# Transposes moved into the next quad's first product, and operand loads held back behind a deep transfer queue

## The chip, the cores and the metric

The kernel runs on one core of a Trainium2 chip. Its time is the device time of one execution in microseconds (us). A core has five engines that run side by side, each with its own instruction stream in order: PE multiplies matrices into PSUM, DVE does elementwise work on whole tensors, ACT does elementwise functions (and copies with a scale), POOL here mostly starts transfers that add while they write, and SP starts the plain transfers. PE's weight loads stand in the profile as a stream of their own (PEld). An instruction that needs another engine's result, or a buffer that another engine still reads, waits at the head of its stream, and everything behind it waits with it.

## The reference

One layer of an encoder trunk over 512 tokens of 2048 channels, in float32: an adaLN modulation computed from c, a token mixer (an RG-LRU group and a pooling group), and a SwiGLU network with 5632 hidden channels. The part that the change touches is the last one:

```
h = modulate(rmsnorm(x, g_norm_ffn), sh2, sc2)
f = (silu(h @ w_ffn_gate) * (h @ w_ffn_up)) @ w_ffn_down
x = x + gt2[:, None, :] * f
return rmsnorm(x, g_norm_final)
```

## The kernel before

Every float32 matrix is split into two parts that PE can multiply fast, `hi` (rounded) and `lo` (the rest), and a product takes three matmuls: hi·hi, hi·lo, lo·hi (`mm3x`). On top of that, the feed-forward products use a Strassen-like scheme with seven block products in place of eight (`seven`, line 876). The function runs seven products one after the other; the steps are called P1, G5, G6, G3, G7, P2, G4 after each product's evacuation. For each product, `parts_of` makes the `hi` on ACT and the `lo` on DVE from a weight tile or from a sum of weight tiles, in 3 buffers each.

The gate and up projections are done in 11 *quads* (NFF = 11), each of 512 hidden channels of both weights. In a quad one product has 4 steps i of 12 matmuls (2 k, 2 row tiles, 3 terms), so 48 matmuls of 512 columns, and a quad has 336. P1's product is the first of a quad, G4 the last. `gate_up` (line 996) turns the results into four tiles of f: C11 (two tiles, ready after P2) and C21 (two tiles, ready only after G4: ACT takes silu of G4's PSUM banks, DVE multiplies). `keep` (line 1033) then transposes f with 16 PE transposes in two rounds of 8 (two PSUM tiles `mm` of four transposes each per round; there are two `mm` buffers, so the second round needs what the first wrote to have been read), builds the seven operand parts of each round by ACT and DVE (`operands`, line 855), and stores them to DRAM (`f_kept`, 14 stores of 256 KB a quad).

The down projection is done in four blocks (2, 3, 3, 3 quads of hidden channels). At the start of a block the operand parts are loaded back into tiles of tag `blk` (line 1056), 28 loads of 256 KB for the first block and 42 for each later one. There are 69 `blk` buffers. The operands of the first block are loaded while the last quad of gate and up still runs.

The order of all instructions comes from a planner (`Program`). Each operation is recorded, gets a due time (`deadlines`: PE's operations at their place in the recorded order, others backwards from what needs them), and `schedule` then plays the program through with fixed costs of its own. At each step it takes, per engine, the operation that could start first, and among equals the one that is due first; PE may run ahead of its recorded order by at most AHEAD = 40 us. `buffers` decides whether an operation that needs a new buffer may take it now. Where a recorded operation stands in the program so sets only its due time, and the planner may still move it.

All instructions are issued from line 356, so the profile's rows are told apart by tile names: `acc` and `mm` are PSUM tiles, `raw` and `araw` weight tiles in SBUF (`araw` is also the running sum of weights), `b` the `blk` tiles, `f` the stored operands.

Of the kernel before, what the change touches and what calls it, by code (L numbers as in the profile page):

```python
# [36 lines left out]
class Program:  # L37
# [21 lines left out]
    AHEAD = 40.0  # L59
    RAW_AHEAD = 50.0  # L60
    SPARE_AHEAD = 40.0
    SCAN = 8

    class Queue:
# [139 lines left out]
    def schedule(self):  # L204
# [55 lines left out]
        def buffers(op, now):  # L260

            need, when = [x[0] for x in op["w"] if x[0] in tags and x[0] not in taken], 0.0
            for name in need:
                tag = tags[name]
                late = op["due"] - shift - now
                if not free[tag] or tag == "raw" and late > self.RAW_AHEAD and not wide:
                    return need, None
                if not fits(name, self.spare.get(tag, 0) if late > self.SPARE_AHEAD else 0):
                    return need, None
                when = max(when, min(free[tag]))  # L270
            return need, when
# [88 lines left out]
def hybrid_trunk(ctx: ExitStack, tc: tile.TileContext, a: dict, out: bass.AP):  # L360
# [512 lines left out]
        return {"A11": (a11[:, 0:H], a11[:, H:T]), "n1": two(s1h, s1l, 0), "s2": two(s1h, s1l, 1), "n4": two(s2h, s2l, 0),  # L873
                "n3": two(s2h, s2l, 1), "A12": two(fh, fl, 0), "A22": two(fh, fl, 1)}

    def seven(left, b, after, by_dma, by_tile=False):


        n = len(left) // 2
# [2 lines left out]
        def product(name, bank, start, stop, right):  # L882
            if start:
                banks[bank] = [mmps("acc") for _ in range(2)]
            for i in range(n):
                product_of(banks[bank], left[2 * i:2 * i + 2], name, right(i), range(2), start and i == 0, stop and i == n - 1)

        def product_of(bank, pairs, name, right, tiles, start, stop):
            for k in range(2):
                lh, ll = pairs[k][name]  # L890
                for j in tiles:
                    cols = slice(j * P, (j + 1) * P)
                    mm3x(bank[j], (lh[:, cols], ll[:, cols]), (right[0][:, k, :], right[1][:, k, :]),
                         start and k == 0, stop and k == 1)
# [76 lines left out]
    left = []  # L971
# [21 lines left out]

    gt2_part = gt2_steps()

    def gate_up(n):
        got = {}

        def after(step, banks):
# [27 lines left out]
        def b(i, row, column):  # L1027
            return (wg, wu)[column][:, 4 * i + 2 * row:4 * i + 2 * row + 2, n * 512:(n + 1) * 512]

        seven(left, b, after, True)  # L1030
        return [got["C11", 0], got["C11", 1], got["C21", 0], got["C21", 1]]

    def keep(n, f):
        for i in range(2):
# [5 lines left out]
            nc.scalar.activation(out=full1, in_=ft[0], func=AF.Copy)  # L1040
            operands(full1, ft[1], f_kept[2 * n + i])

    for n in range(NFF):
        keep(n, gate_up(n))


    fsum = [[None] * 4 for _ in range(NT)]
# [2 lines left out]
    for bi, nb in enumerate(DOWN_BLOCKS):  # L1050
# [15 lines left out]
        for qp in range(2):  # L1066
# [95 lines left out]
            if last and qp:  # L1162
                for t in (2, 3):
                    residual(t, qa)
            seven(left, b, later_block if bi else first_block, False, by_tile=last and qp == 1)
        n0 += nb

    nc.issue()
# [22 lines left out]
```

## Time and profile before

| | us |
|---|---|
| runs shown, median of 3 | 1891.26 |
| lowest, highest | 1891.05, 1896.01 |
| the profiled execution's own time | 1895.01 |
| its span, first to last instruction | 1893.1 |
| PE busy in the span | 1806.1 (95%) |
| DVE busy | 1539.7 (81%) |
| DMA engines, mean rate | 227 GB/s |

The gate and up quads run from about 580 to 1447 us of the span, one every 79 us; the down blocks run from there to the end. An engine's busy time says how full it is, not what waits for it. Where PE is close to full, what matters is the few gaps in its stream, and the rows of waits say what ended each.

### The profile page before, as it was taken

How to read it: one execution, taken by the hardware profiler on the slowest of the kernel's cores; microseconds unless marked ns; L12 is line 12 of the kernel's file. 1: busy time of each engine (PE TensorE's matmuls, PEld its weight loads, DVE VectorE, ACT ScalarE, POOL GpSimd, SP SyncE). 2: the span in 40 equal slices, each digit the busy share in tenths (PEclk: the TensorE clock that was granted, in tenths of full speed). 3: DMA queues.
4: the chain of work that ended last, by engine and by line, in shares of the span. 5: the costliest groups of instructions: out<-in, count | busy, mean ns of one | idle time of the engine just before them, and what ended most of it. 6: DMA issues, size and time to landing. Idle time of an engine off the chain costs nothing.

```text
span 1893.1 us, 22786 instructions
## 1 busy us (share of the span) xinstructions
PE 1806.1 (95%) x8011; PEld 1473.2 (78%) x8011; DVE 1539.7 (81%) x1974; ACT 936.4 (49%) x1221; POOL 197.4 (10%) x192
## 2 busy tenths in 40 slices
PE   3899999899999999999999999999999999999996
PEld 2687877688887888888888788787887888888875
DVE  5898998889969878678787867877667887888888
ACT  7434684422377545454554544545445543333345
POOL 0000054500001111111111111111110000000011
PEclk9999999999999999999999999999999999999999
DMA  9999755499954778788868877876799765947566
GB/s 297 312 349 292 237 183 178 141 327 318 364 168 97 189 201 222 202 211 219 226 180 217 224 191 208 221 194 183 169 291 341 245 232 186 354 143 261 195 155 164
DMA packets 285763, 429.97 MB, mean 227 GB/s; under 512 B 20760, under 2 KB 119760, under 8 KB 285648
## 3 DMA queue, kind: packets, MB, share of 16 engines
q1 hardware_dynamic: 259408, 378.17, 59.9%
q0 software_dynamic: 26240, 50.34, 15.9%
q8 instruction: 63, 1.03, 0.2%
q14 instruction: 52, 0.43, 0.1%
HBM read 378.63 MB, written 49.81 MB: 226 GB/s over the span
## 4 chain that ended last, share of the span: by engine, by line
PE 64%; DVE 14%; DMA 9%; issue 8%; ACT 3%; POOL 1%; SPq 1%; ACTq 0%; DVEq 0%; POOLq 0%
PE acc L356 62%; DVE b L356 10%; DVE lo L356 4%; DMA araw<-in_w_ada 3%; PE mm L356 2%; ACT b L356 2%; DMA raw<-in_w_ada 1%; ACT hi L356 1%; DMA raw<-in_w_ffn_up 1%; DMA araw<-in_w_ffn_up 1%; SPq L356 1%; DMA araw<-in_w_ffn_gate 1%; DMA raw<-in_w_out 0%; DMA f<-b 0%; DMA raw<-in_w_in 0%
## 5 line engine op out<-in xcount | busy, mean ns | idle before, releaser
L356 PE MATMUL acc<-hi,b 128*128 128x512 f32 x4208 | 1271.4, 392 | 5.3 <-ACT hi L356 2.2
L356 PEld LDWEIGHTS acc<-hi,b 128*128 128x128 f32 x4208 | 789.6, 189 | 169.8 <-ACT hi L356 7.6
L356 PE MATMUL acc<-lo,b 128*128 128x512 f32 x2104 | 782.9, 393 | 4.4 <-DVE lo L356 4.3
L356 ACT ACTIVATE hi<-raw 128x1024 fp32r<-128x1024 f32 (+2 forms) x297 | 306.6, 1035 | 447.2 <-PE acc L356 362.5
L356 DVE TENSOR_TENSOR lo<-raw,hi 128x1024 fp32r<-128x1024 f32 (+2 forms) x297 | 356.1, 1202 | 148.4 <-ACT hi L356 144.1
L356 PEld LDWEIGHTS acc<-lo,b 128*128 128x128 f32 x2104 | 396.1, 189 | 91.5 <-DVE lo L356 10.9
L356 ACT ACTIVATE hi<-araw 128x1024 fp32r<-128x1024 f32 x264 | 279.7, 1060 | 283.1 <-PE acc L356 257.5
L356 DVE TENSOR_TENSOR lo<-araw,hi 128x1024 fp32r<-128x1024 f32 x198 | 241.5, 1220 | 58.2 <-ACT hi L356 57.5
L356 DVE SCALAR_TENSOR_TENSOR b<-araw,c_act,b 128x512 f32<-128x512 f32 (+1 forms) x315 | 232.0, 741 | 11.3 <-DMA araw<-in_w_ada 8.0
L356 DVE TENSOR_TENSOR b<-b,b 128x512 f32<-128x512 f32 (+4 forms) x318 | 194.3, 633 | 13.7 <-ACT b L356 11.3
L356 PE MATMUL acc<-b,hi 128*128 128x512 f32 x608 | 191.4, 400 | 5.0 <-ACT b L356 2.1
L356 ACT ACTIVATE b<-b 128x512 fp32r<-128x512 f32 (+2 forms) x223 | 128.6, 597 | 106.1 <-DVE b L356 64.9
L356 PEld LDWEIGHTS acc<-b,hi 128*128 128x128 f32 x608 | 115.9, 192 | 32.4 <-ACT b L356 4.3
L356 PE MATMUL acc<-b,lo 128*128 128x512 f32 x304 | 116.7, 398 | 2.5 <-DVE lo L356 2.5
L356 POOL DMA_DIRECT2D araw<-in_w_ffn_up x44 | 53.1, 1206 | 586.7 <-DVE lo L356 412.1
L356 ACT ACTIVATE b<-acc 128x512 f32<-128x512 f32 x142 | 82.1, 594 | 57.6 <-PE acc L356 42.6
L356 DVE SCALAR_TENSOR_TENSOR lo<-araw,hi 128x1024 fp32r<-128x1024 f32 x66 | 80.5, 1220 | 34.4 <-ACT hi L356 34.1
L356 DVE TENSOR_TENSOR araw<-araw,raw 128x1024 f32<-128x1024 f32 x88 | 106.7, 1219 | 0.8
L356 POOL DMA_DIRECT2D raw<-in_w_ffn_up x44 | 53.0, 1204 | 317.7 <-DVE lo L356 290.2
L356 DVE SCALAR_TENSOR_TENSOR araw<-araw,raw 128x1024 f32<-128x1024 f32 x66 | 79.9, 1219 | 6.9 <-DMA raw<-in_w_ffn_down 3.5
L356 PE MATMUL mm<-b,hi 128*128 128x512 f32 x192 | 62.1, 404 | 10.3 <-ACT b L356 10.3
L356 PEld LDWEIGHTS acc<-b,lo 128*128 128x128 f32 x304 | 58.5, 192 | 16.0 <-DVE lo L356 3.8
(72 smaller groups left out, 868.2 us busy)
## 6 DMA issues: line engine op xcount, KB each, us to landing
araw<-in_w_ada SPq DMA_DIRECT2D x256, 256.0 KB, 4.7
raw<-in_w_ffn_down SPq DMA_DIRECT2D x88, 512.0 KB, 5.3
f<-b SPq DMA_DIRECT2D x154, 256.0 KB, 3.7
b<-f SPq DMA_DIRECT2D x154, 256.0 KB, 6.0
araw<-in_w_ffn_gate SPq DMA_DIRECT2D x44, 512.0 KB, 3.8
raw<-in_w_ffn_up SPq DMA_DIRECT2D x44, 512.0 KB, 4.5
araw<-in_w_ffn_up POOLq DMA_DIRECT2D x44, 512.0 KB, 6.6
raw<-in_w_ffn_gate SPq DMA_DIRECT2D x44, 512.0 KB, 4.9
```

Of the source, the lines that this page charges most:

```text
L356: getattr(getattr(self.nc, queue), method)(*args, **kw)
```

## The change

Two edits. In `seven` a new argument `within` is called in the midst of the first product ("A11", step i = (n-1)//2): after 24 of its matmuls have been recorded in a quad, after 12 in the first block of the down projection. The transposes and operand work of quad n (`keep`) are no longer recorded behind quad n, but handed to quad n+1 as `within`, and those of the last quad to the first product of the first down block. In `buffers` a transfer that would take a new `blk` buffer is held back while the planner's own transfer queue is more than DMA_AHEAD = 4 us deep, unless it is already due.

```diff
--- before.py
+++ after.py
@@ -59,6 +59,7 @@
     AHEAD = 40.0
     RAW_AHEAD = 50.0
     SPARE_AHEAD = 40.0
+    DMA_AHEAD = 4.0
     SCAN = 8
 
     class Queue:
@@ -264,6 +265,8 @@
                 tag = tags[name]
                 late = op["due"] - shift - now
                 if not free[tag] or tag == "raw" and late > self.RAW_AHEAD and not wide:
+                    return need, None
+                if op["dma"] and tag == "blk" and dma_free - now > self.DMA_AHEAD and late > 0.0 and not wide:
                     return need, None
                 if not fits(name, self.spare.get(tag, 0) if late > self.SPARE_AHEAD else 0):
                     return need, None
@@ -873,7 +876,8 @@
         return {"A11": (a11[:, 0:H], a11[:, H:T]), "n1": two(s1h, s1l, 0), "s2": two(s1h, s1l, 1), "n4": two(s2h, s2l, 0),
                 "n3": two(s2h, s2l, 1), "A12": two(fh, fl, 0), "A22": two(fh, fl, 1)}
 
-    def seven(left, b, after, by_dma, by_tile=False):
+    def seven(left, b, after, by_dma, by_tile=False, within=None):
+
 
 
         n = len(left) // 2
@@ -884,6 +888,8 @@
                 banks[bank] = [mmps("acc") for _ in range(2)]
             for i in range(n):
                 product_of(banks[bank], left[2 * i:2 * i + 2], name, right(i), range(2), start and i == 0, stop and i == n - 1)
+                if within and name == "A11" and i == (n - 1) // 2:
+                    within()
 
         def product_of(bank, pairs, name, right, tiles, start, stop):
             for k in range(2):
@@ -993,7 +999,7 @@
 
     gt2_part = gt2_steps()
 
-    def gate_up(n):
+    def gate_up(n, within):
         got = {}
 
         def after(step, banks):
@@ -1027,7 +1033,7 @@
         def b(i, row, column):
             return (wg, wu)[column][:, 4 * i + 2 * row:4 * i + 2 * row + 2, n * 512:(n + 1) * 512]
 
-        seven(left, b, after, True)
+        seven(left, b, after, True, within=within)
         return [got["C11", 0], got["C11", 1], got["C21", 0], got["C21", 1]]
 
     def keep(n, f):
@@ -1040,8 +1046,10 @@
             nc.scalar.activation(out=full1, in_=ft[0], func=AF.Copy)
             operands(full1, ft[1], f_kept[2 * n + i])
 
+    kept = None
     for n in range(NFF):
-        keep(n, gate_up(n))
+        f = gate_up(n, kept)
+        kept = lambda n=n, f=f: keep(n, f)
 
 
     fsum = [[None] * 4 for _ in range(NT)]
@@ -1162,7 +1170,7 @@
             if last and qp:
                 for t in (2, 3):
                     residual(t, qa)
-            seven(left, b, later_block if bi else first_block, False, by_tile=last and qp == 1)
+            seven(left, b, later_block if bi else first_block, False, by_tile=last and qp == 1, within=kept if not bi and not qp else None)
         n0 += nb
 
     nc.issue()

```

What this does to the order shows at three places. The first is PE at the end of quad 4 (gate and up; counted from 0). `acc1385/1386` (before) and `acc1361/1362` (after) are the last product G4, `b983` and the like are parts of h, `mm1473/1474` and `mm1481/1482` the first round's transposed f, made from C11 (`b1401`, `b1402`) and C21 (`b1471`, `b1472`). Before:

```order
L356 MATMUL acc1386_1511<-hi1468_1593,b1052_1151 128x512
L356 MATMUL mm1473_1598<-ident_68,b1401_1526 128x128
L356 MATMUL mm1473_1598<-ident_68,b1402_1527 128x128
L356 MATMUL mm1474_1599<-ident_68,b1401_1526 128x128
L356 MATMUL mm1474_1599<-ident_68,b1402_1527 128x128
L356 MATMUL acc1497_1622<-hi1500_1625,b983_1082 128x512
L356 MATMUL acc1497_1622<-lo1501_1626,b983_1082 128x512
L356 MATMUL acc1497_1622<-hi1500_1625,b983_1082 128x512
L356 MATMUL acc1498_1623<-hi1500_1625,b983_1082 128x512
L356 MATMUL acc1498_1623<-lo1501_1626,b983_1082 128x512
L356 MATMUL mm1473_1598<-ident_68,b1471_1596 128x128
```
After; in front of these rows stand 14 more matmuls of the next quad's first product, which follow G4's last matmul directly:

```order
L359 MATMUL acc1473_1598<-hi1479_1604,b1001_1100 128x512
L359 MATMUL mm1481_1606<-ident_68,b1401_1526 128x128
L359 MATMUL acc1474_1599<-hi1479_1604,b1001_1100 128x512
L359 MATMUL mm1481_1606<-ident_68,b1402_1527 128x128
L359 MATMUL mm1481_1606<-ident_68,b1471_1596 128x128
L359 MATMUL acc1474_1599<-lo1480_1605,b1001_1100 128x512
L359 MATMUL mm1481_1606<-ident_68,b1472_1597 128x128
L359 MATMUL mm1482_1607<-ident_68,b1401_1526 128x128
L359 MATMUL acc1474_1599<-hi1479_1604,b1001_1100 128x512
L359 MATMUL mm1482_1607<-ident_68,b1402_1527 128x128
L359 MATMUL acc1473_1598<-hi1479_1604,b1010_1109 128x512
L359 MATMUL mm1482_1607<-ident_68,b1471_1596 128x128
```
The first transpose of a C21 tile moved from behind 5 matmuls and 4 transposes to behind 16 matmuls and 2 transposes, counted from the last matmul of G4.

The second place is the same boundary a little later on PE, where the second round takes the `mm` buffers again. `mm1486` (before) takes the buffer of `mm1474`; `mm1494` (after) takes that of `mm1482`. Before:

```order
L356 MATMUL mm1485_1610<-ident_68,b1472_1597 128x128
L356 MATMUL acc1498_1623<-hi1500_1625,b992_1091 128x512
L356 MATMUL acc1497_1622<-hi1503_1628,b1001_1100 128x512
L356 MATMUL acc1497_1622<-lo1504_1629,b1001_1100 128x512
L356 MATMUL acc1497_1622<-hi1503_1628,b1001_1100 128x512
L356 MATMUL acc1498_1623<-hi1503_1628,b1001_1100 128x512
L356 MATMUL acc1498_1623<-lo1504_1629,b1001_1100 128x512
L356 MATMUL acc1498_1623<-hi1503_1628,b1001_1100 128x512
L356 MATMUL acc1497_1622<-hi1503_1628,b1010_1109 128x512
L356 MATMUL acc1497_1622<-lo1504_1629,b1010_1109 128x512
L356 MATMUL mm1486_1611<-ident_68,b1401_1526 128x128
```
After:

```order
L359 MATMUL acc1474_1599<-hi1479_1604,b1010_1109 128x512
L359 MATMUL mm1493_1618<-ident_68,b1401_1526 128x128
L359 MATMUL mm1493_1618<-ident_68,b1402_1527 128x128
L359 MATMUL mm1493_1618<-ident_68,b1471_1596 128x128
L359 MATMUL mm1493_1618<-ident_68,b1472_1597 128x128
L359 MATMUL acc1473_1598<-hi1506_1631,b1019_1118 128x512
L359 MATMUL acc1473_1598<-lo1507_1632,b1019_1118 128x512
L359 MATMUL acc1473_1598<-hi1506_1631,b1019_1118 128x512
L359 MATMUL mm1494_1619<-ident_68,b1401_1526 128x128
```
Between the last transpose of the second PSUM tile and the first of the fourth stood 13 matmuls and 4 transposes, and stand now 8 matmuls and 4 transposes. At every second boundary there were 11 matmuls and 4 transposes; now all ten have 8 and 4. The last transpose of the first PSUM tile and that of the second stood next to each other; now four transposes and two matmuls further apart.

The third place is PE at the end of the last quad. `b2183`, `b2184` are C11, `b2249`, `b2250` C21, `acc2303/2304` (before) and `acc2279/2280` (after) the first product of the first down block. Before:

```order
L356 MATMUL acc2170_2295<-hi2247_2372,b1052_1151 128x512
L356 MATMUL mm2251_2376<-ident_68,b2183_2308 128x128
L356 MATMUL mm2251_2376<-ident_68,b2184_2309 128x128
L356 MATMUL mm2252_2377<-ident_68,b2183_2308 128x128
L356 MATMUL mm2252_2377<-ident_68,b2184_2309 128x128
L356 MATMUL mm2251_2376<-ident_68,b2249_2374 128x128
L356 MATMUL mm2252_2377<-ident_68,b2249_2374 128x128
L356 MATMUL mm2251_2376<-ident_68,b2250_2375 128x128
L356 MATMUL mm2252_2377<-ident_68,b2250_2375 128x128
L356 MATMUL mm2263_2388<-ident_68,b2183_2308 128x128
L356 MATMUL mm2263_2388<-ident_68,b2184_2309 128x128
L356 MATMUL mm2263_2388<-ident_68,b2249_2374 128x128
```
After:

```order
L359 MATMUL acc2146_2271<-hi2247_2372,b1052_1151 128x512
L359 MATMUL mm2284_2409<-ident_68,b2183_2308 128x128
L359 MATMUL acc2279_2404<-hi2282_2407,b2251_2376 128x512
L359 MATMUL mm2284_2409<-ident_68,b2184_2309 128x128
L359 MATMUL mm2284_2409<-ident_68,b2249_2374 128x128
L359 MATMUL acc2279_2404<-lo2283_2408,b2251_2376 128x512
L359 MATMUL mm2285_2410<-ident_68,b2183_2308 128x128
L359 MATMUL acc2279_2404<-hi2282_2407,b2251_2376 128x512
L359 MATMUL mm2285_2410<-ident_68,b2184_2309 128x128
L359 MATMUL acc2280_2405<-hi2282_2407,b2251_2376 128x512
L359 MATMUL mm2285_2410<-ident_68,b2249_2374 128x128
L359 MATMUL acc2280_2405<-lo2283_2408,b2251_2376 128x512
```
Before, 12 transposes stand in one piece between the last matmul of the gate and up quads and the first of the down projection; now matmuls of the down projection stand between them from the second row on.

On SP, during the last quad, 26 loads of stored operands (`b<-f`) stood ahead of the load of `raw2235`, a gate weight tile of that quad; now 13 do, and the rest comes behind the first weight tiles of the down projection (`raw2315` and those after it). The number of loads is the same.

## Rows read from the trace of the kernel before

**Rows 1.** The page's busy time: engine, us busy, share of span, instructions
```profile
...
PE 1806.1 (95%) x8011; PEld 1473.2 (78%) x8011; DVE 1539.7 (81%) x1974; ACT 936.4 (49%) x1221; POOL 197.4 (10%) x192
```

**Rows 2.** Waits of PE from 650 to 1446: us in total, times, longest
```profile
...
PE mm L356 <- DVE b L356: 4.8, 7, 1.6
PE acc L356 <- DVE lo L356: 1.3, 2, 0.8
```

**Rows 3.** Timeline of PE, 888 to 893: start, length, what, in brackets idle before
```profile
...
889.86 0.63 PE L356 MATMUL acc<-hi,b 128*128 128x512 f32 x2
890.33 0.39 PE L356 MATMUL acc<-lo,b 128*128 128x512 f32 x1
891.67 0.44 PE L356 MATMUL mm<-ident,b 128*128 128x128 f32 x2 [0.96 <-DVE b L356]
```

**Rows 4.** Timeline of DVE, 887 to 896
```profile
...
889.79 1.22 DVE L356 SCALAR_TENSOR_TENSOR lo<-araw,hi 128x1024 fp32r<-128x1024 f32 x1
890.92 1.29 DVE L356 TENSOR_TENSOR b<-b,b 128x512 f32<-128x512 f32 x2
```

**Rows 5.** Timeline of ACT, 886 to 896
```profile
...
888.47 1.28 ACT L356 ACTIVATE b<-acc 128x512 f32<-128x512 f32 x2 [0.53 <-PE acc L356]
```

**Rows 6.** Windows: length, busy us of each engine (x instructions), PEclk, DMA share, GB/s
```profile
658.00:1291.00 633.00, 628.37 (x2827) 517.80 (x2826) 492.48 (x570) 322.05 (x389) 77.15 (x65) 1.00 0.79 208
1291.00:1446.00 155.00, 153.15 (x675) 123.98 (x674) 105.67 (x116) 73.26 (x88) 15.64 (x13) 1.00 0.85 245
888.00:902.00 14.00, 13.04 (x65) 10.39 (x65) 13.77 (x22) 8.84 (x14) 3.64 (x4) 1.00 0.92 186
1446.00:1460.00 14.00, 12.10 (x44) 8.60 (x43) 11.31 (x16) 8.07 (x12) 0.00 (x0) 0.76 1.04 374
1452.00:1458.00 6.00, 6.00 (x17) 4.64 (x18) 6.00 (x7) 2.44 (x4) 0.00 (x0) 0.56 1.05 402
385.00:450.00 65.00, 65.00 (x295) 54.05 (x294) 60.48 (x86) 19.31 (x27) 1.63 (x1) 1.00 0.95 319
```

**Rows 7.** Timeline of PE, 812 to 818
```profile
...
812.31 0.38 PE L356 MATMUL mm<-ident,b 128*128 128x128 f32 x2
...
815.06 0.63 PE L356 MATMUL acc<-hi,b 128*128 128x512 f32 x2
815.90 0.63 PE L356 MATMUL mm<-ident,b 128*128 128x128 f32 x4 [0.21 <-DVE b L356]
```

**Rows 8.** Instructions on tile mm from 700 to 1446: ns min/median/max
```profile
...
L356 PE MATMUL mm<-ident,b x144: 269/272/332, 731.9 to 1372.2; 128*128 128x128 f32 x144
L356 DVE TENSOR_TENSOR b<-mm,b x40: 408/680/685, 736.1 to 1386.1; 128x512 fp32r<-128x512 f32 x18, 128x256 f32<-128x256 f32 x18, 128x512 f32<-128x512 f32 x4
L356 ACT ACTIVATE b<-mm x36: 576/591/601, 734.5 to 1373.2; 128x512 f32<-128x512 f32 x18, 128x512 fp32r<-128x512 f32 x18
```

**Rows 9.** Timeline of PE, 1440 to 1462
```profile
...
1448.27 0.43 PE L356 MATMUL mm<-ident,b 128*128 128x128 f32 x2 [0.24 <-DVE b L356]
1449.28 0.65 PE L356 MATMUL mm<-ident,b 128*128 128x128 f32 x4 [0.58 <-ACT b L356]
1450.71 1.22 PE L356 MATMUL acc<-hi,b 128*128 128x512 f32 x2 [0.78 <-ACT hi L356]
```

**Rows 10.** DMA issues from 1212 to 1288: count, KB each, median us to landing
```profile
...
raw<-in_w_ffn_up POOLq DMA_DIRECT2D x4, 512.0 KB, 6.4
```

**Rows 11.** DMA issues from 1370 to 1446
```profile
...
b<-f SPq DMA_DIRECT2D x47, 256.0 KB, 5.9
...
raw<-in_w_ffn_up POOLq DMA_DIRECT2D x4, 512.0 KB, 11.9
```

**Rows 12.** Waits of all engines from 1370 to 1460
```profile
...
ACT hi L356 <- DMA raw<-in_w_ffn_up: 11.0, 4, 3.4
```

**Rows 13.** Waits of all engines over the whole span
```profile
...
ACT b L356 <- DMA f<-b: 5.5, 2, 4.9
```

## The prediction

> **What bounds the kernel now.** I began with the page's busy times: PE computes in 95% of the span, DVE in 81% [rows 1]. A kernel this full on PE is shortened by fewer matmuls or smaller gaps between them, and the change leaves the number of matmuls as it is. So I looked for the gaps in the part that the change touches. The windows give them: in the quads from 658 to 1291, 628.37 of 633 us are busy, from 1291 to 1446 153.15 of 155 [rows 6]. Together 6.5 us are lost, and the waits of PE over the same stretch account for 6.1 of them: 4.8 in transposes (`mm`) that wait for DVE, in 7 gaps, and 1.3 in two matmuls that wait for a `lo` [rows 2].
>
> The timelines say what the waits are. At 891.67 PE starts the first transpose of a C21 tile 0.96 late [rows 3]. Its operand is made by the two multiplies that DVE starts at 890.92 [rows 4]; ACT's silu of the G4 banks starts at 888.47 and takes 1.28 for two [rows 5], so about 889.8 the multiplies could have run, but DVE started a `lo` split of 1.22 at 889.79, and streams run in order. There is a second kind: at 815.90 the first transpose of the second round is 0.21 late, again for DVE, though its f tiles had been there for long [rows 7]. What it waits for is its PSUM buffer, since there are two `mm` buffers and DVE must have read the old one.
>
> The last boundary is worse. From 1446 to 1460 PE moves 44 instructions, where the same length of an ordinary boundary, 888 to 902, moves 65 [rows 6]. Three waits of 0.24, 0.58 and 0.78 [rows 9] follow one another, and then comes a stretch of 6 us with a granted clock of 0.56 in which 17 instructions pass [rows 6]: most of it is at the lower of the two levels, 1.2 GHz. A single wait of up to 1.6 us, as in the quads [rows 2], left the clock at 1.00 [rows 6].
>
> **A: the ten boundaries between quads.** The idle times understate the loss. From 890.33 to 891.67 are 1.34 us [rows 3], and a matmul of 512 columns takes 0.235 of the stream (0.47 between 889.86 and 890.33 for two [rows 3]), so the delay is 1.1 where the row says 0.96. With 0.15 more for each of 7 gaps the loss is 4.8 + 1.05 = 5.9.
>
> After the change the first C21 transpose stands behind 16 matmuls and 2 transposes of G4's successor. A transpose takes 0.12 of the stream ((0.63 - 0.27) / 3 for four [rows 7, 8]), so it comes 16 x 0.235 + 0.24 = 4.0 us behind G4's end. The multiplies need 1.28 of silu, up to 1.22 of a split and 1.29 for themselves, with parts of these overlapping; in the worst case 3.8. This wait goes.
>
> What is late next is the release of `mm`. In the row of 812 the last transpose of the second tile starts at 812.31 + 0.11, and the buffer is free at 815.90: 3.5 us [rows 7]. That is two ACT copies of 0.59 one after the other and five or six DVE steps of 0.41 to 0.68 [rows 8]. Now only 8 matmuls and 4 transposes stand between, 1.9 + 0.5 = 2.4 us, where 11 or 13 matmuls stood (3.1 or 3.5). With the chain unchanged the wait would be 1.1 at each boundary. But the first PSUM tile is now complete four transposes and two matmuls before the second instead of at the same time, 0.95 where 0.1 was, so its copy starts some 0.85 earlier, and if the whole chain follows, it ends 3.5 - 0.85 = 2.65 behind the second tile: a wait of 0.25. I take 0.3, nearer to this end because the copies are what starts the chain. Ten boundaries: 3.0 us. A gains 5.9 - 3.0 = 2.9. The bounds: no wait at all, +5.9; 1.2 at each boundary, 12, -6.1.
>
> The operand work of a quad stands about 4 us later on DVE and ACT. DVE is busy for 492.48 of 633 [rows 6], so 22% is free, and I take 0; if a `lo` of the running product is pushed behind it, that costs up to one split, 1.22, where it happens. The tiles are also held longer, so copies may wait for the stores of f: 0, with 4.9, the longest such wait of ACT [rows 13], as the upper bound.
>
> **B: loads held back.** In the quad from 1212 to 1288 the adding loads of `raw` on POOL land after 6.4 us [rows 10]; from 1370 to 1446, with 47 loads of `b<-f` beside them, after 11.9 [rows 11], and ACT waits 11.0 us in all for them [rows 12]. This stretch has the two PE waits for `lo` [rows 2], 1.3 + 2 x 0.15 = 1.6. With the loads thinned out to 13 in front of the last gate weights instead of 26, I expect them gone: +1.6. Bounds: 0, if the transfers only come at another time, and 1.85, all that PE lacks from 1291 to 1446 [rows 6]; what the held loads may cost is the second rival.
>
> The Trainium skill ("DMA: Bandwidth & Descriptors", section "Rules for kernel authors") advises to issue the DMA early, to compute, and to wait on its semaphore late. This speaks against holding loads back that have buffers; the trace of before speaks for it here, with 6.4 us become 11.9 in the stretch with the early loads. By the rule B would be nothing, or the second rival.
>
> **C: the last boundary.** Against the ordinary boundary 65 - 44 = 21 instructions are missing from 14 us, 21 x 0.235 = 4.9, and the ordinary one contains a wait of 1.1 itself: 6.0 us lost, with the lower clock in it. Now first-block matmuls stand between the transposes, and the three waits of [rows 9] have work to cover them; so no run of short waits and, I expect, no drop of the clock. Its `hi` and `lo` come earlier, ahead of the silus and multiplies. I leave 1.1 for the release of `mm` or a first operand that is late. C gains 4.9. Bounds: 0, if the first product's operands are the limit; 6.0.
>
> **Elsewhere.** In the token mixer the order of loads changes too, but PE is busy 65.00 of 65 us at a DMA share of 0.95 [rows 6]: 0, with 2 us to either side for what a late tile could do. In the down projection behind its first block PE's order stays as it was: 0.
>
> **Sum.** 2.9 + 1.6 + 4.9 = 9.4 us. The profiled execution took 1895.01 (its span is 1893.1), so 1885.6 by this sum. It stands 3.75 above the median of the runs shown, 1891.26; from the median the sum gives 1881.9. Part of the 3.75 may be the very stalls of B and C, so I start from the middle of the two, 1893.1, and forecast 1883.7.
>
> **Rival 1: the waits only move to `mm`.** Chain 3.5, cover 2.4, so 1.1 to 1.2 at each boundary: 12 us where 5.9 were, and A becomes -6.1. With B and C the sum is 0.4, and the time 1893.1 - 0.4 = 1892.7: no change. For it speaks that the release already ended a wait with 11 matmuls in front [rows 7], and there are fewer now; against it the head start of the first copy. 0.2.
>
> **Rival 2: the held loads come late.** This is the case that ends slower. The first down block needs 28 loads; 15 of them now stand among the weight tiles of the down projection on SP, and a DMA share of 1.04 from 1446 to 1460 at 374 GB/s [rows 6] says that the queue is full there already. 15 x 0.262 MB and as many MB of weights are some 8 MB, 21 us at that rate, while each of the block's seven products, 24 matmuls on 4 such loads, takes 5.6 us. If an operand lands as late as a weight tile does, one landing of 11.9 [rows 11], PE stands for that once, and the clock falls: 17 instructions in 6 us [rows 6] against 25 at full rate, 2 us lost. 14 us, from 1883.7 to 1897.7. It decides from the point where PE stands 13.2 us in all for such loads. Against it: what is held is only held until it is due, and the parts of the first product are among the 13 that go first. By the skill's rule above this would be the expected end; no row of before shows a `b<-f` load that PE waited for. 0.12.
>
> **Rival 3: the second edit does nothing.** B is 0 and C is halved since the last quad's late `raw` tiles still set when the silus run: 2.9 + 2.5 = 5.4, and 1887.7, within the bound of no change. 0.15.
>
> **How the numbers follow.** A difference under 0.3%, 5.7 us, can't be told from none here; so faster is below 1885.6, slower above 1896.9. My forecast with its own spread has 0.53: its time, 1883.7, is 2 us below the limit, A alone may shift it by 3 either way, so some 0.35 of it is faster with room, 0.1 near the limit and counted as faster, the rest as no change. Rivals 1 and 3 are no change, apart from their better halves that reach below the limit (0.1). Faster 0.55, no change 0.33, slower 0.12. The range: at the lower end A without any wait and C in full, 5.9 + 1.85 + 6.0 = 13.75 from the lower starting point, 1877.5, and 2 for the mixer, 1875.5; at the upper end rival 1 with a part of B or C missing, 1894.
>
> **What would show it.** A: in the changed trace, the waits of PE for DVE on `mm` from 650 to 1446; about 3 in all at ten places, all of them at the first transpose of a second round and none at a C21 tile. If they sum to 8 or more, rival 1 is right. B: landing of the adding loads near 6 to 8 us in the last quad, and no PE wait for `lo`. C: in 14 us around the last quad's end more than 60 PE instructions and a granted clock of 1.00. Rival 2 would show as a PE wait for DMA `b<-f` behind 1446. I'm wrong if the gain lies outside the boundaries, or if the quads as a whole get slower though their PE waits shrink.

## The result

The changed kernel takes 1873.03 us, the kernel before 1891.55 in the same comparison: a ratio of 0.9902, interval 0.988 to 0.9923. So it is faster, as forecast, by 18.5 us where 9.4 were worked out, and 1873.03 lies below the range. Two more comparisons of the same pair (e4 and e10 below) gave 0.9932 (0.991 to 0.9953) and 0.9895 (0.9877 to 0.9912). The size is thus some 13 to 21 us. Single executions of the kernel before lie between 1885 and 1900 us, so the size of a gain this small is known only roughly.

The profile after, first the busy times (as [rows 1]) and the waits of PE over the quads, 639 to 1440 (as [rows 2]):

```profile
...
PE 1797.6 (96%) x8011; PEld 1469.1 (79%) x8011; DVE 1540.0 (82%) x1974; ACT 935.9 (50%) x1221; POOL 196.3 (11%) x192
```

```profile
...
PE acc L359 <- DVE lo L359: 0.5, 1, 0.5
```

The waits for DVE at transposes, 4.8 us before, have gone in this trace, and of the two waits for `lo`, 1.3, neither is left; the one of 0.5 is at another place (933 us). A second trace of the changed kernel (e4 below) has two waits at transposes again, at one boundary. The timeline of PE at the quad boundary near 725 (start, length, what; it answers to [rows 3, 7]):

```profile
...
724.10 0.39 PE L359 MATMUL acc<-hi,b 128*128 128x512 f32 x1
724.34 0.27 PE L359 MATMUL mm<-ident,b 128*128 128x128 f32 x1
...
724.68 0.38 PE L359 MATMUL mm<-ident,b 128*128 128x128 f32 x2
...
725.13 0.38 PE L359 MATMUL mm<-ident,b 128*128 128x128 f32 x2
...
728.23 0.40 PE L359 MATMUL acc<-hi,b 128*128 128x512 f32 x1
728.67 0.63 PE L359 MATMUL mm<-ident,b 128*128 128x128 f32 x4
```

The transposes of the first round stand one or two at a time between matmuls of the next quad, and no bracket shows idle time. What is left of the release of `mm` is the step from 728.23 to 728.67, 0.44 where 0.23 would be the matmul alone. The windows over the quads and the 14 us behind the last of them (columns as [rows 6]):

```profile
...
645.00:1277.00 632.00, 631.14 (x2838) 519.31 (x2837) 494.45 (x570) 322.01 (x390) 78.27 (x65) 1.00 0.79 209
1277.00:1428.00 151.00, 151.00 (x679) 124.48 (x678) 108.76 (x121) 75.99 (x93) 15.64 (x13) 1.00 0.83 238
1425.00:1439.00 14.00, 14.00 (x71) 11.45 (x70) 12.88 (x16) 10.63 (x16) 0.00 (x0) 1.00 0.94 338
```

From 645 to 1428 PE lacks 0.9 us, where it lacked 6.5. At the last boundary it moves 71 instructions in 14 us at a granted clock of 1.00; before it moved 44 at 0.76. And the adding loads in the last quad (transfers issued from 1350 to 1426; count, size, median us to landing, as [rows 11]):

```profile
...
b<-f SPq DMA_DIRECT2D x30, 256.0 KB, 6.2
...
raw<-in_w_ffn_up POOLq DMA_DIRECT2D x4, 512.0 KB, 6.5
```

They land after 6.5 us, not 11.9, with 30 loads of `b<-f` beside them in place of 47.

To see where the time went in all, I counted PE's instructions (8011 in every trace) and took the time between the starts of the same numbers. "Before" and "changed" have three traces each; "held only" and "transposes only" are the experiments e1 and e2.

| PE instructions | what runs there | before | held only | transposes only | changed |
|---|---|---|---|---|---|
| 0 to 2400 | adaLN, token mixer | 601.7, 600.7, 597.0 | 600.3 | 598.6 | 590.8, 594.6, 594.1 |
| 2400 to 5500 | quads | 696.1, 693.1, 697.1 | 694.8 | 691.3 | 692.9, 693.8, 691.6 |
| 5500 to 5700 | quads, last but one boundary | 47.1, 47.2, 47.8 | 47.4 | 45.3 | 45.3, 45.3, 45.3 |
| 5700 to 6050 | to the end of the last quad | 79.9, 79.8, 80.1 | 78.7 | 79.6 | 77.7, 77.8, 77.8 |
| 6050 to 6200 | last boundary | 38.3, 37.0, 38.0 | 32.3 | 34.7 | 32.3, 32.3, 32.3 |
| 6200 to 8010 | down projection, end | 417.8, 418.2, 419.6 | 417.8 | 417.6 | 417.5, 417.0, 416.9 |

The first row counts from the span's start. As means of three: the quads gain 695.4 - 692.8 = 2.6, the two last-quad rows 127.3 - 123.1 = 4.2, the last boundary 37.8 - 32.3 = 5.5, together 12.3; the end gives 1.4 and the beginning 6.6, of which more below. That is 20.3 in these traces, each of one execution; the comparison above gave 18.5.

### The profile page after: what moved, and what is told of

It is laid out like the page before. It is cut to its first block, busy times and chain, and to the rows that moved or that the text cites. A ratio compares the mean times of both kernels' runs of the same rounds, so it can differ in the third digit from the quotient of the medians.

```text
span 1868.9 us, 22751 instructions
## 1 busy us (share of the span) xinstructions
PE 1797.6 (96%) x8011; PEld 1469.1 (79%) x8011; DVE 1540.0 (82%) x1974; ACT 935.9 (50%) x1221; POOL 196.3 (11%) x192
## 3 DMA queue, kind: packets, MB, share of 16 engines
q8 instruction: 63, 1.03, 0.2%
## 4 chain that ended last, share of the span: by engine, by line
PE 65%; DVE 15%; issue 9%; DMA 7%; ACT 2%; SPq 1%; POOL 1%; ACTq 0%; DVEq 0%; POOLq 0%
PE acc L359 62%; DVE b L359 10%; DVE lo L359 4%; DMA araw<-in_w_ada 3%; PE mm L359 3%; ACT b L359 2%; SPq L359 1%; DVE araw L359 1%; DMA b<-x 1%; DMA raw<-in_w_ffn_down 1%; ACT hi L359 1%; DMA b<-in_x 1%; DMA araw<-in_w_ffn_up 1%; DMA raw<-in_w_ffn_gate 0%; DMA araw<-in_w_ffn_gate 0%
## 5 line engine op out<-in xcount | busy, mean ns | idle before, releaser
L359 PE MATMUL acc<-hi,b 128*128 128x512 f32 x4208 | 1290.0, 392 | 1.6 <-DVE b L359 1.0
L359 PE MATMUL acc<-lo,b 128*128 128x512 f32 x2104 | 803.1, 393 | 4.7 <-DVE lo L359 4.5
L359 DVE SCALAR_TENSOR_TENSOR lo<-araw,hi 128x1024 fp32r<-128x1024 f32 x66 | 80.6, 1223 | 47.6 <-ACT hi L359 47.4
L359 DVE SCALAR_TENSOR_TENSOR araw<-araw,raw 128x1024 f32<-128x1024 f32 x66 | 79.9, 1220 | 13.6 <-DMA raw<-in_w_ffn_gate 8.6
L359 POOL DMA_DIRECT2D raw<-in_w_ffn_up x44 | 53.0, 1204 | 334.4 <-DVE lo L359 332.9
```

The lines of the kernel that those rows point to most:

```text
L359: getattr(getattr(self.nc, queue), method)(*args, **kw)
```

## The experiments

**e1, only the held loads.** The transposes follow their quad as before.

```
     for n in range(NFF):
         f = gate_up(n, kept)
-        kept = lambda n=n, f=f: keep(n, f)
+        keep(n, f)
```

> Only the holding back of loads; the transposes stay behind their quad as before. Theory 1 (each edit acts in its own places): the two waits for lo in the last quads go (the traces put 3.8 us there), and the wait for sh at 469.81 of before with the slow clock behind it (3.0 us), so about 7 us less than before, ratio 0.996; the waits of PE for DVE at the transposes stay at 4 to 5 us, and the 14 us around the last boundary still move fewer than 50 PE instructions. Rival: the loss at the last boundary (6.0 us) came from the crowded queue, not from the place of the transposes; then it goes here too, about 13 us less, ratio 0.993, and those 14 us move 60 or more.

Ratio 0.9942 (0.9924 to 0.996). At the ordinary boundaries the waits stay (7 at transposes, 3.6 us), but the last boundary is as quick as in the changed kernel. Theory 1 fell on this point, and the rival held. Theory 1 was wrong on two more: both waits for `lo` stayed (0.8 and 0.6 us), and so did the wait for `sh`, 1.1 us. The windows of PE instructions 6050 to 6200, first the kernel before (its third trace), then e1:

```profile
...
1422.00:1460.00 38.00, 35.22 (x151) 27.88 (x151) 27.65 (x34) 17.61 (x24) 0.00 (x0) 0.96 1.03 369
```

```profile
...
1421.20:1453.40 32.20, 32.20 (x151) 26.58 (x150) 26.41 (x31) 17.74 (x24) 0.00 (x0) 1.00 0.96 351
```

38.0 us against 32.2, without any transpose moved by hand. The reason shows on SP's queue. The first tile `araw` of the down projection's weights, from which the first `hi` is made, is issued at these times (start, length, engine, what), before and in e1:

```profile
...
1438.89 1.00 SPq L356 DMA_DIRECT2D araw<-in_w_ffn_down  x2
```

```profile
...
1429.37 0.38 SPq L359 DMA_DIRECT2D araw<-in_w_ffn_down  x1
```

From PE's instruction 6050 that is 1438.89 - 1422.0 = 16.9 us on in the one and 1429.37 - 1421.2 = 8.2 in the other. SP issues in order, and before, the load stood behind 44 loads of `b<-f` in its order, in e1 behind 26. The planner plays this queue through: with the weight late it wrote 12 transposes in one piece at the last boundary, with the weight in time it puts matmuls of the down projection between them, though nothing in the program asks for it. That the one is the reason of the other is read from the two orders and these times; an earlier weight with all loads of `b<-f` in their old places wasn't run.

**e2, only the transposes.** No load is held back.

```
-                if op["dma"] and tag == "blk" and dma_free - now > self.DMA_AHEAD and late > 0.0 and not wide:
+                if False and op["dma"] and tag == "blk" and dma_free - now > self.DMA_AHEAD and late > 0.0 and not wide:
```

> Only the transposes inside the next quad's first product; no load is held back. Theory 1: the ten boundaries give 3.0 us and the last boundary 6.0, together 9 less, ratio 0.995; the wait for sh near 470 and the two waits for lo in the last quads stay. Rival (the last boundary's loss belongs to the crowded queue): 3 us less, ratio 0.998, and a stretch at the lower clock behind the last quad.

Ratio 0.9963 (0.995 to 0.9976), between the two expectations. The quads give what they give in the changed kernel (691.3), the last boundary 3.1 of the 5.5 us (window of PE instructions 6050 to 6200):

```profile
...
1414.90:1449.60 34.70, 33.27 (x152) 26.66 (x151) 25.76 (x31) 16.56 (x21) 0.00 (x0) 1.00 0.97 366
```

That is 34.7 us, with the first `araw` issued 13.9 us behind instruction 6050, and 8 of the 16 transposes again in one piece, 4 more two matmuls behind them. The stretch at the lower clock that the rival expected isn't there. e2 also shows which edit cures the first of the two waits for `lo`: instructions 5500 to 5700 take 45.3 as in the changed kernel, where e1 needs 47.4. That wait had not come from the adding loads. ACT's timeline of the kernel before at this place:

```profile
...
1303.35 0.60 ACT L356 ACTIVATE b<-acc 128x512 f32<-128x512 f32 x1 [4.95 <-DMA f<-b]
1303.84 2.00 ACT L356 ACTIVATE hi<-araw 128x1024 fp32r<-128x1024 f32 x2
```

The evacuation of the product, `b<-acc`, stood 4.95 us for a store `f<-b` that still read the buffer it writes; the `hi` behind it on ACT was late, so `lo` was, so PE. The same wait of ACT over instructions 5500 to 5700 (us in total, times, longest), in e1, e2 and the changed kernel:

```profile
...
ACT b L359 <- DMA f<-b: 5.2, 1, 5.2
```

```profile
...
ACT b L359 <- DMA f<-b: 1.2, 1, 1.2
```

```profile
...
ACT b L359 <- DMA f<-b: 1.3, 1, 1.3
```

Moving the operand work 4 us on takes this wait from 5.2 to 1.2, and holding loads does nothing for it. The second wait for `lo`, in the last quad, is the one for late adding loads; their landing there in e1 and e2:

```profile
...
raw<-in_w_ffn_up POOLq DMA_DIRECT2D x4, 512.0 KB, 10.9
```

```profile
...
raw<-in_w_ffn_up POOLq DMA_DIRECT2D x4, 512.0 KB, 11.6
```

Neither edit alone brings the landing down from 11.9 (10.9 and 11.6), and each alone leaves a wait of 0.5 to 0.6; in the changed kernel it is 6.5, and the wait is gone. That both edits are there is not enough: e8 below has both, with 20 loads of `b<-f` ahead of `raw2235` as in e1, and its adding loads land after 11.3 and leave a wait of 0.4. With 13 ahead they land after 6.5 to 8.0 (three traces), with 19 (e9) after 8.7, with 26 (before) after 11.9.

**e3, the kernel before once more, and e4, the changed one once more.**

> The kernel before, once more, for a second trace of its first 300 us. In the first pair of traces the changed kernel is 7.8 us ahead by PE's instruction 1000 (270.4 against 262.6), though PE, DVE and ACT have the same order there. Theory 1: most of that is what executions of one kernel differ by; the second trace reaches instruction 600 at 170 to 174 in place of 175.9, without the wait of 1.68 at 151.41. Rival: the four rows in SP's order (the load of w_conv behind five loads of w_ada) make it; then the second trace stands within 1 us of the first, at 175 to 177.

> The changed kernel, once more, on the same chip as the single edits. Both theories: ratio 0.990 to 0.991. PE's instruction 600 lies at 169 to 172 if the order of SP sets the first 300 us, and anywhere from 169 to 175 if executions differ there.

e4 gave 0.9932 (0.991 to 0.9953), less of a gain than the 0.990 to 0.991 expected. Instruction 600 came at 172.6 in e3 and at 171.3 in e4, and the wait at the place of 151.41 is in both, 1.7 us. So the expectation on that wait was wrong, and the time to instruction 600 differs between executions of one order: over all traces 170.9 to 175.9 with the order of before, 168.9 to 175.6 with that of the change.

e4's quads hold something that the first trace of the changed kernel doesn't show. Waits of PE from 590 to 1440, then the row of DVE at the place, both e4:

```profile
...
PE mm L359 <- DVE b L359: 2.0, 2, 1.5
```

```profile
...
727.81 0.75 DVE L359 SCALAR_TENSOR_TENSOR b<-raw,c_act,b 128x512 f32<-128x512 f32 x1 [3.33 <-DMA raw<-in_w_ada]
```

Both waits stand at one boundary, near 730: 0.5 at a C21 transpose and 1.5 at the second round. DVE had stood 3.33 us just before for a tile of `w_ada`, from which adaLN parts are still computed during the quads. What this says of the kernel before comes under A.

**e5, only `b<-f` is held, with the transposes; e6, only the other loads are held, without them.**

```
+        op["kept"] = op["dma"] and kw["in_"].tensor.name.startswith("f")
...
-                if op["dma"] and tag == "blk" and dma_free - now > self.DMA_AHEAD and late > 0.0 and not wide:
+                if op["dma"] and tag == "blk" and op["kept"] and dma_free - now > self.DMA_AHEAD and late > 0.0 and not wide:
```

In e6 `op["kept"]` is `not op["kept"]`, and `keep` follows its quad as in e1.

> The changed kernel, but only the loads of stored operands (b<-f) are held back; the other blk loads (x, w_conv, biases) go out as in the kernel before. PE's order is the changed kernel's. Theory 1: what the change gives from PE's instruction 2400 to 6200 (10.5 us by the traces so far: 859.2 as the mean of two of before, 848.8 of two of after) is all that there is, the first 600 us being the same but for chance; then this kernel stands with the changed one within the interval, ratio 0.993 to 0.994, with 848 to 850 in that stretch. Rival: the held loads of x and others give another 3 to 5 us in the first 600 us; then this one stands 0.002 to 0.003 behind the changed one, at 0.9945 to 0.996.

> The kernel before, with only the blk loads that are not b<-f held back. PE's order is that of before. Theory 1: no difference, ratio 0.999 to 1.001, and instruction 2400 reached at 598 to 602 as in the three traces without the held loads. Rival: 3 to 5 us less, ratio 0.997 to 0.9985, instruction 2400 at 591 to 597, with the wait for sh in the mixing stage under 0.8 where it was 1.3, 1.6 and 2.1. In the last quads nothing changes by either.

e5: 0.9935 (0.9921 to 0.9948), with 847.0 us from instruction 2400 to 6200: all of the change's gain in its own stretch. e6: 0.9992 (0.998 to 1.0003), the ratio of theory 1, but with instruction 2400 at 596.0 and no wait for `sh`, as the rival had it. The two don't agree on what the loads of x and others are worth. By e6 it is 1.6 us, with an interval from a gain of 3.8 to a loss of 0.6. e5, which does without it, stands level with e4 (0.9932) but some 0.003 to 0.004 behind the two other comparisons of the changed kernel (0.9902 and 0.9895), all on other chips. What the traces add comes under "Elsewhere".

**e7, the two rounds of transposes set apart.**

```
-                if within and name == "A11" and i == (n - 1) // 2:
-                    within()
+                if within and name == "A11" and i in ((n - 1) // 2, (n - 1) // 2 + 1):
+                    within(i - (n - 1) // 2)
```

> The changed kernel, with the two rounds of transposes set apart: the first after step 1 of the next quad's first product, the second after step 2 (0 and 1 in the first down block). If the small remainders at the boundaries (0.17 to 0.22 at each second round, 2 us over ten) and the lo waits of up to 0.7 come from two rounds close together on two mm buffers, 2 to 3 us less than the changed kernel, ratio 0.9915 to 0.992. Rival: the operand work of the second round now falls later, onto the splits of the next products, and what the release gives back comes again as waits for lo: no difference from the changed kernel.

Ratio 0.9978 (0.9966 to 0.9991): slower than the changed kernel, which neither theory nor rival expected. PE's waits from 580 to 1480, and the timeline at one of them:

```profile
...
PE acc L359 <- ACT b L359: 8.6, 4, 2.1
```

```profile
...
832.12 0.39 PE L359 MATMUL acc<-hi,b 128*128 128x512 f32 x1
834.66 0.80 PE L359 MATMUL acc<-hi,b 128*128 128x512 f32 x1 [2.15 <-ACT b L359]
```

ACT's timeline there:

```profile
...
832.55 1.06 ACT L359 ACTIVATE hi<-araw 128x1024 fp32r<-128x1024 f32 x1 [1.66 <-PE acc L359]
833.51 0.61 ACT L359 ACTIVATE b<-b 128x512 fp32r<-128x512 f32 x1
834.03 2.04 ACT L359 ACTIVATE b<-acc 128x512 f32<-128x512 f32 x4
```

Behind four of the ten boundaries PE stands once 2.1 us for an `acc` bank that ACT has not yet evacuated: a split and a copy stand in front of the evacuation, which starts at 834.03 and frees PE at 834.66. Behind the wait the clock falls (0.72 granted from 834 to 840). The quads take 704.1 us, 11 more than in the changed kernel, of which 8.6 are these waits. A place for work inside a product was good here only where its ACT work kept out of the way of the next evacuation.

**e8, one step earlier.**

```
-                if within and name == "A11" and i == (n - 1) // 2:
+                if within and name == "A11" and i == 0:
```

> The changed kernel, with the transposes recorded after step 0 of the first product in a quad, not after step 1. The first transpose of a C21 tile stands behind about 6 matmuls and 5 transposes of G4's end (2.0 us, where the change has 4.0 and before had 1.7), the second round's last tile behind 16 matmuls and 4 transposes (4.2 us, where the change has 2.4). Theory on the boundaries: the wait for C21 comes back, 0.5 to 1.1 at seven or more boundaries, 5 to 7 us in all, and the remainders of 0.17 to 0.22 at the second rounds go (2 us); instructions 2400 to 5500 take 694 to 697, where the changed kernel took 691.6 to 693.8; ratio 0.995 to 0.9965. Rival: the release of mm set the pace, C21 would be in time here too; then 690 to 691, ratio 0.9925.

The waits of PE from 590 to 1440, then the timeline of PE at the longest and that of DVE in front of it, and of PE at one of the others:

```profile
...
PE mm L359 <- DVE b L359: 3.0, 6, 1.4
```

```profile
...
728.20 0.27 PE L359 MATMUL mm<-ident,b 128*128 128x128 f32 x1
728.23 0.47 PE L359 MATMUL acc<-hi,b 128*128 128x512 f32 x1
730.09 0.44 PE L359 MATMUL mm<-ident,b 128*128 128x128 f32 x2 [1.39 <-DVE b L359]
```

```profile
...
726.08 1.54 DVE L359 SCALAR_TENSOR_TENSOR b<-raw,c_act,b 128x512 f32<-128x512 f32 x2 [2.12 <-DMA raw<-in_w_ada]
```

```profile
...
969.11 0.62 PE L359 MATMUL acc<-hi,b 128*128 128x512 f32 x2
970.07 0.63 PE L359 MATMUL mm<-ident,b 128*128 128x128 f32 x4 [0.33 <-DVE b L359]
```

Only the longest of the six waits is at a C21 tile, and there DVE had stood 2.12 us for `w_ada`. The other five, 0.3 each, are at the second round, for the release of `mm`. Counting as late what the step to a transpose takes beyond the usual 0.23 (behind a matmul) or 0.12 (behind a transpose), idle time or not, they are 0.47 to 0.49 late there at every second boundary and not at all at the rest, 2.4 us together, where the changed kernel has 0.15 to 0.21 at each of ten, 1.8 together. So neither half of the theory held: the waits for C21 didn't come back at seven boundaries, and the release of `mm` came to cost no less. The quads take 694.0 us, where the changed kernel's three traces have 691.6 to 693.8, and the whole kernel, 0.9922 (0.9901 to 0.9943), can't be told from the changed one.

**e9, holding above 8 us.** DMA_AHEAD = 8.0.

> The changed kernel, with loads held back above 8 us of queue in place of 4: 19 loads of b<-f before raw2235 where there are 13 (26 without holding), 29 before the first araw tile of the down projection; PE's order at the last boundary nearly that of the changed kernel (matmuls between the transposes). Theory: what costs time at the last boundary is the order alone that the planner writes when it sees the weight tile late; then instructions 6050 to 6200 take 32.3 to 32.6 here too, ratio 0.993. Rival: the weight tile's landing on the chip decides; it is issued behind 16 loads more, and PE waits for it in this order, 34 to 36 for the stretch, ratio 0.9945.

Ratio 0.9939 (0.992 to 0.9958), and 32.3 us for the last boundary, as the theory said. But it doesn't decide between theory and rival: the first `araw` is issued at 1421.55, 8.2 us behind instruction 6050 as in the changed kernel, although it stands behind more loads. Whether PE would have waited for a later landing stays open.

**e10 and e11, both kernels a third time.**

> The changed kernel a third time, for its size: the first comparison gave 0.9902 (0.988 to 0.9923), the second 0.9932 (0.991 to 0.9953). Theory: the change is worth what its own stretch shows, 10 to 12 us, and the first comparison stood high by the chance of its few executions; then 0.993 to 0.9945, and instructions 2400 to 6200 take 848 to 850. Rival: 18 us is the true size and part of it lies in the first 600 us; then 0.9895 to 0.991.

> The kernel before a third time, for a third trace. Theory: instruction 2400 is reached anywhere from 596 to 602, as in the traces of all the kernels; 2400 to 6200 take 857 to 861. Rival: 2400 at 600 or later, as in both earlier traces of before, so that the changed kernel's 590.8 and 594.6 are its own.

e10: 0.9895 (0.9877 to 0.9912), against my theory. Two of the three comparisons now stand near 0.990 and one at 0.9932, so 18 us is nearer to the size than 12. e11 reached instruction 2400 at 597.0, as the theory allowed, and took 863.0 from there to 6200, 2 us above it, with 137.9 us for instructions 4600 to 5200 where the two other traces of before need 134.9 and 134.0. In this stretch PE stands 2.95 us for a C21 tile, and the clock falls behind it (0.79 granted from 1204 to 1212); DVE had stood 2.77 us for `w_ada`. So the kernel before doesn't lose the same in each execution.

## Why the forecast was right in direction and too small

**Which step failed.** The time lies 2.5 us below the range. The terms for the boundaries and the last quad, A, B and C, came to 12.3 in the traces, less than the 13.75 that the range allowed them; from 1891.55 they alone would give 1879.3, inside it. The step that failed is "Elsewhere": "PE is busy 65.00 of 65 us ...: 0, with 2 us to either side". The traces show 8.0 us there, 6.6 before instruction 2400 and 1.4 behind 6200, and only about 2 of them have a likely cause. By the forecast's own sign, that I'm wrong if the gain lies outside the boundaries, this part of it was wrong. B was mis-sized as well, 1.6 for 4.2, and C was given to the wrong edit.

**A, the boundaries: the number right, the account in part wrong.** 2.9 forecast, 2.6 measured. I had read DVE's timeline [rows 4] from the `lo` split on. The row in front of it, in the kernel before:

```profile
...
887.55 2.33 DVE L356 SCALAR_TENSOR_TENSOR b<-raw,c_act,b 128x512 f32<-128x512 f32 x3 [1.02 <-DMA raw<-in_w_ada]
```

DVE stood 1.02 us for a tile of `w_ada`, and all behind it on DVE, the split and the two multiplies, came late. The same holds wherever a C21 transpose is more than 0.2 late (counted as under e8) in the traces with the old place of the transposes (three of before, e1, e6), twelve times in all: the lateness is DVE's wait for `w_ada` and about 0.1 more (1.02 and 1.11, 1.43 and 1.53, 1.71 and 1.79 in the first trace). Where DVE doesn't stand for `w_ada` at a boundary, C21 is in time. So the new place gives cover for a weight that lands late: with 4.0 us of it, waits of DVE up to 1.0 leave no wait of PE at C21, 3.33 in e4 does; with the 2.0 of e8, 0.47 leaves none and 2.12 does. This is read from the traces; a run with the loads of `w_ada` out of the way wasn't made. It also means that the 5.9 from which I started belongs to one execution. The same sum is 2.9 and 5.2 in the two other traces of before, and that the forecast and the measured gain agree so well is in part luck.

The release of `mm` did not take the place of these waits. It makes the transposes 0.15 to 0.21 late at each of ten boundaries, 1.8 us in all where 3.0 was put down. In the kernel before it cost as much, 0.38 at four boundaries and 0.16 at two. Rival 1 would have shown 12 us of waits. There are none in two traces of the changed kernel, and 2.0 at one boundary in e4.

**C, the last boundary: right in size, wrong in cause.** 4.9 forecast, 5.5 measured. The step "now first-block matmuls stand between the transposes" gave this to the transposes' edit. e1 has it in full without that edit, and e2 only in part. What goes with the matmuls between the transposes is the weight tile that is issued 8.7 us earlier relative to PE. I read the order of the changed kernel as a whole and did not ask which edit made which row. Rival 3 (the second edit does nothing, C halved) did not come: the second edit alone gives C in full. Its halved C, 2.5, is near the 3.1 of e2, which is without the second edit.

**B, the held loads: mis-sized in its own stretch.** The step was +1.6, with at most 1.85, "all that PE lacks from 1291 to 1446 [rows 6]"; the two rows of the table give 4.2. The bound failed since a busy share hides losses: matmuls are shown with 0.39 us each while they follow one another every 0.23, so a delay of up to 0.16 leaves no idle time at all. I had added this for the gaps that had a row, not for the many that had none. The cause was half right. Late adding loads stood behind one of the waits, the one of the last quad, where the changed kernel gains 2.2 us and the held loads alone 1.2. The other, worth 2.1, was ACT's wait for a store, and e2 shows that it goes with the transposes' edit, not with the held loads. That was [rows 13], which I had taken for the upper price of the change, and it was a loss that the change removes.

**Elsewhere: put at nothing, and not settled.** The step rested on one window, 385 to 450, in which PE has no gap. Twenty us behind its end, still in the token mixer, PE waits in the kernel before for `sh`, and the clock falls; the first trace of the changed kernel has neither. The timeline of PE in the kernel before, then 10 us around the wait there and around the same place in the changed kernel (columns as [rows 6]):

```profile
...
469.81 0.47 PE L356 MATMUL mm<-b,ones_r 128*128 128x512 f32 x1 [1.26 <-DVE sh L356]
```

```profile
...
465.00:475.00 10.00, 8.74 (x39) 7.21 (x38) 9.96 (x17) 1.06 (x1) 0.00 (x0) 0.83 0.95 312
```

```profile
...
457.00:467.00 10.00, 10.00 (x51) 8.48 (x51) 9.57 (x17) 1.06 (x1) 0.00 (x0) 1.00 1.00 328
```

How much of the 6.6 us before instruction 2400 belongs to the change, the other traces help to tell. Up to there e2, e5 and e9 run in the order of the kernel before on all five engines (e9 too: above 8 us of queue no load of x is held), and e1, e6, e7 and e8 in that of the changed kernel. The six traces with the old order need 595.0 to 601.7, the seven with the new one 590.8 to 600.3; the means, 598.6 and 595.5, differ by 3.1. In the first 600 instructions PE, DVE and ACT have one order, and the means differ by 0.7. In the mixing stage (instructions 1700 to 1900), where the order on DVE differs, the six take 44.6 to 47.4 us and the seven 43.5 to 46.4, 1.9 less in the mean; the wait for `sh` is 0.9 to 2.1 in all six, and in the seven it is at most 1.1 and absent in two. So a gain of about 2 us in the mixing stage is likely. The ratios of whole kernels don't settle it: e6 puts the loads of x at 1.6 us, with zero inside its interval; the two kernels with both other gains but the old order at the start, e5 and e9, have 0.9935 and 0.9939, where the changed kernel has 0.9902, 0.9932 and 0.9895. What makes up the rest of the 6.6, and the 1.4 at the end, stays open.

**Base.** I started from 1893.1, between the profiled execution and the median of the runs shown; the median of the comparison was 1891.55. That put the forecast 1.5 us too high.

**Rival 2: did not come.** From 1400 us to the end the changed kernel's three traces show no wait of PE for a load. The Trainium skill's advice ("DMA: Bandwidth & Descriptors", "Rules for kernel authors") to issue a DMA early spoke for this rival; here an earlier issue of the stored operands pushed a weight that was needed sooner 8.7 us back in the same queue, and issuing them later gave e1 its 5.5 us at the last boundary.

## What to carry to other kernels

When a change has two edits and an order is planned by a program, look at the order with each edit alone before giving a term to one of them. Take the loss of a stretch from the starts of the same instructions, or from a stretch without waits, not from the busy share of a pipelined engine, and from more than one trace where a late load stands behind it. When an engine is late, read its timeline back to the last row in which it stood for something. A load that is issued because the queue's engine has nothing better to do isn't free: ask what is next behind it in that queue.

## What the runs showed of the hardware beside this

In the beginning of the kernel executions of the same order on all five engines differ by up to 6.7 us to PE's instruction 2400 (595.0 to 601.7, six traces); the DMA share there is 0.97 to 0.99 over the first 600 instructions and 1.03 to 1.05 in the mixing stage of these traces. In the down projection, from instruction 6200 to 7700, all thirteen traces agree within 1.6 us in about 341 (340.4 to 342.0).
